# A mixture of 32 experts in another order: 64 slots from place 8 on, heavy and light groups in turn, the last scatter behind the branch

## The chip, the core and the metric

The kernel runs on one core of a Trainium2 chip, as one program in one launch. The metric is the time of one execution on the device in microseconds; the median of a few executions is quoted. Profiles show one execution, with times counted from its first instruction.

## What is computed

One layer of a decoder trunk on 256 tokens of width 1024: an attention mixer, a normalisation, then a mixture of experts and a second normalisation. All data are 32-bit floats. The change lies in the mixture:

```python
def moe_ffn(h, router_w, router_b, w_gu, b_gu, w_down, b_down):
    tok = h.reshape(Bn * S, D)                     # 256 x 1024
    logits = (tok @ router_w + router_b)           # 256 x 32
    top_v, top_i = lax.top_k(logits, TOP_K)        # 4 of 32 experts
    top_w = jax.nn.softmax(top_v, axis=-1)
    combine = jnp.sum(jax.nn.one_hot(top_i, N_EXPERTS) * top_w[..., None], axis=1)
    for e in range(N_EXPERTS):
        gu = tok @ w_gu[e] + b_gu[e]               # 1024 x 2048
        gate = jnp.minimum(gu[:, 0::2], SWIGLU_LIMIT)
        up = jnp.clip(gu[:, 1::2], -SWIGLU_LIMIT, SWIGLU_LIMIT)
        act = (up + 1.0) * (gate * jax.nn.sigmoid(SWIGLU_ALPHA * gate))
        out = out + combine[:, e:e + 1] * (act @ w_down[e] + b_down[e])   # 1024 x 1024
    return out
# x = layer_norm(DN_ALPHA * x + (1.0 + gate) * moe_ffn(...), ln2_g, ln2_b)
```

The 1024 pairs of token and expert are spread unevenly. With the reference's drawn inputs, experts 0 and 1 get 18 and 2 tokens, and the other thirty, sorted by count, get 84, 82, 70, 69, 68, 65, 55, 46, 42, 41, 38, 34, 33, 31, 31, 29, and then from 25 down to 6.

## The kernel before

**Weights.** Every expert has 12 MB of weights, which `Stream` loads as 12 units of 1 MB, each into one buffer of 128 x 2048 floats (`Stream.unit`, L121). All loads are issued on SP's queue, in the order in which the experts are computed. In the mixture the buffers are taken in turn from the list `ROUND`, which names 3 + 2 + 5 + 4 + 1 + 1 + 1 = 17 of them (`FIRST`, `ROUND`); the four of `PARTS` are those that `W.place` gives. A load waits on SP until TensorE has done with the unit that the same buffer held 17 loads earlier.

**Slots and places.** The tokens of one expert are gathered into slots, whose number is fixed when the program is built. Experts 0 and 1 are computed first, with 64 slots each (group `G0`). The others are sorted on the chip by their token counts: place 2 is the fullest. `slots_of(p)` gives a place 128, 64 or 32 slots: class `Wide` for places 2 to 8 (`WIDE = 9`), `Narrow` for 9 to 15, `Few` for 16 to 31. A `Wide` expert streams each weight column through the whole array, a `Narrow` one runs two products beside each other on half of the columns, a `Few` one four on a quarter each. If any expert has more tokens than slots, a flag is set (`order[32]`), and behind the last expert all engines enter the branch `tc.If(more[0] > 0)` (L1711), which computes the experts once more for the tokens left over. Otherwise they jump over it.

**Groups.** Two experts make a group, which gathers its tokens together (`Group.gather`, four times four products from `xr` through `sel`, while the group before it is still computed), and turns and weighs its slots (`slots`, `weights`). Within a group the second member is computed first. A *heavy* group is one `Wide` and one `Narrow` place, a *light* one two `Few` places. `sweep` walks through 24 steps for each expert; tables of steps (`first`, `side`, `turn`) hold what is done beside the weight products. The order of the groups is written out:

```python
groups = [G0]
for heavy in (0, 1, 1, 0, 1, 1, 0, 1, 1, 0, 1, 0, 0, 0, 0):
```

TensorE, SP and GpSimd issue in the order of the program text, and so do VectorE and ScalarE in the mixture.

**The end.** Each expert's result is scaled by its weights (`weigh`, to `y`) and added by a product with `selT` to the sums `acc` in PSUM (`scatter`, on step 25 counted from the expert's start). Before the last expert, `first_sum` moves the sums so far, scaled by one plus the gate, into `x1`; the last expert starts the sums afresh and is scaled by the gate in `weigh` (`late`, `first_of_all`). The gate and the two rows of the last normalisation are spread over 128 partitions by small products with a row of ones (`spread_row`, `keep_row`) into two of the buffers of `W.place`, which `W.keep` takes out of the list. Behind the branch VectorE adds `acc` to `x1` (L1734) and the last normalisation follows.

Of the kernel before, what the change touches and what calls it, by code (L numbers as in the profile page):

```python
# [17 lines left out]
D = 1024  # L18
# [9 lines left out]
WIDE = 9  # L28
# [51 lines left out]
class Stream:  # L80
# [4 lines left out]
    def __init__(self, nc, pool, ahead):  # L85
# [4 lines left out]
        self.small = None  # L90
# [7 lines left out]
    def keep(self):  # L98

        many = len(self.others)  # L100
        at = next(j for j in ((self.turn + i) % many for i in range(many)) if self.others[j] == self.place)
        self.others = self.others[:at] + self.others[at + 1:]
        self.turn = (self.turn - (at < self.turn)) % len(self.others)
        return self.place()

    def buffer(self):
        if self.others:
            get = self.others[self.turn]
            self.turn = (self.turn + 1) % len(self.others)
            return get()  # L110
        return self.raw()
# [65 lines left out]
def body(tc, A, taps=None):  # L177
# [4 lines left out]
    with ctx:  # L182
# [1007 lines left out]
        class Group:  # L1190
# [12 lines left out]
            def choose(self, engine=POOL):  # L1203
                self.X = [s15("X", (128, 2, 192)) for _ in range(4)]
                self.sel = s2("sel", (128, 2, 256))
                self.selT = [s1("selT", (128, 256)) for _ in self.members]
# [67 lines left out]
        acc = []  # L1274

        class Expert:
# [16 lines left out]
            def weigh(self, y, t, n=None):  # L1293

                z = t2k("y")
# [111 lines left out]
        def late(expert):  # L1407

            return isinstance(expert.key, tuple) or expert.key == experts[-1].key

        def first_of_all(expert):
            return expert.key in (0, experts[-1].key)
# [82 lines left out]
        def sweep(experts, total, base):  # L1495

            for t in range(total + 2):
# [6 lines left out]
                run(turn, t)  # L1504
# [123 lines left out]
        groups = [G0]  # L1628
        for heavy in (0, 1, 1, 0, 1, 1, 0, 1, 1, 0, 1, 0, 0, 0, 0):
            groups.append(Group(pq, [by[128 if heavy else 32].pop(0), by[64 if heavy else 32].pop(0)]))  # L1630
        assert not any(by.values())
        places = [(G, s) for G in groups for s in reversed(range(len(G.members)))]
# [35 lines left out]
        def keep_row(j, n):  # L1668
            b = spread_row(j, n)
            if n == 0 and j != 7:  # L1670
                spread_rows["8" if j == 8 else "67"] = W.keep()
            spread_rows[j] = spread_rows["8" if j == 8 else "67"][:, (j == 7) * D:(j == 7) * D + D]
            spread_rows["g2z"] = spread_rows["8"][:, D:D + 512]
# [155 lines left out]
```

## Time and profile before

| what | us |
|---|---|
| median of 3 runs | 1309.14 |
| fastest and slowest of them | 1307.37 and 1318.86 |
| the profiled execution | 1315.57 |
| its span, first to last instruction | 1313.8 |
| TensorE busy in the span | 1199.0 |
| mixture, first weight product to last | 287.7 to 1295.5 |

The profile's page gives the busy time of each engine, the span in 40 slices, the DMA queues, the chain of work that ended last, and the costliest groups of instructions. Beside the page, the trace was read by windows: the busy time of each engine, the granted TensorE clock (1.00 is 2.4 GHz, 0.50 is 1.2 GHz) and the DMA rate in a stretch. The stretches used here begin and end with the first weight product of a group, so their length is what TensorE took for that group.

### The profile page before, as it was taken

Reading aid. Unit: us, or ns where it says so; the run is one execution under the profiler, and the core shown is the slowest. Engines: PE = TensorE matmul, PEld = TensorE weight load, DVE = VectorE, ACT = ScalarE, POOL = GpSimd, SP = SyncE. Lnnn points to the kernel's source line nnn. Section 1 sums busy time; section 2 is a strip of 40 time slices with the busy share of each in tenths; the row PEclk is TensorE's granted clock in tenths of the full one; section 3 lists DMA queues with packets and bytes.
Section 4 is the critical chain, followed back from the end, with each engine's and each line's share of the span. In section 5 each row is a group of like instructions: output and inputs, shape, how many; then the busy total and the mean of one; then the engine's idle time right before and its main releaser. Section 6 shows DMA issues by size and latency. Waiting matters only on the chain. (4 is left out here: it accounts for less than half of the span.)

```text
span 1313.8 us, 16305 instructions
## 1 busy us (share of the span) xinstructions
PE 1199.0 (91%) x6200; PEld 628.7 (48%) x6200; DVE 405.8 (31%) x937; ACT 277.3 (21%) x546; POOL 90.7 (7%) x120
## 2 busy tenths in 40 slices
PE   6989999989999999988999988999988998787783
PEld 6878888874333444533443533453433353232220
DVE  7898778742122111211111201121211121110023
ACT  4655545331111110111111111111111111110011
POOL 0014620000000000000000000000000000000000
PEclk9999999978999999988999999999999999898887
DMA  9986766929999999799999889999889999999993
GB/s 381 347 334 248 265 222 257 365 83 418 416 420 421 421 421 411 268 374 421 420 370 385 285 340 421 421 414 369 306 319 420 420 420 395 421 420 420 422 417 152
DMA packets 69814, 474.63 MB, mean 361 GB/s; under 512 B 9645, under 2 KB 10346, under 8 KB 13920
## 3 DMA queue, kind: packets, MB, share of 16 engines
q1 hardware_dynamic: 68288, 469.28, 88.9%
q0 software_dynamic: 1296, 3.97, 0.9%
q8 instruction: 51, 0.84, 0.3%
q14 instruction: 35, 0.29, 0.1%
q10 hardware_dynamic: 144, 0.26, 0.1%
HBM read 472.41 MB, written 3.43 MB: 362 GB/s over the span
## 5 line engine op out<-in xcount | busy, mean ns | idle before, releaser
L194 PE MATMUL b<-raw,X 128*32 128x512 f32 (+2 forms) x2048 | 470.1, 608 | 14.1 <-DMA raw<-in_wexp 14.0
L194 PE MATMUL b<-raw,an 128*32 128x512 f32 (+2 forms) x1024 | 256.4, 715 | 43.7 <-DVE an L1388 25.5
L194 PEld LDWEIGHTS b<-raw,X 128*32 128x32 f32 (+2 forms) x2048 | 150.1, 135 | 265.8 <-issue 230.1
L194 PEld LDWEIGHTS b<-raw,an 128*32 128x32 f32 (+2 forms) x1024 | 80.5, 149 | 172.7 <-issue 137.1
L1228 DVE TENSOR_SCALAR X<-b,G,B 128x64 f32<-128x64 f32 (+2 forms) x64 | 26.0, 406 | 412.0 <-ACT X L1230 412.0
L194 PE MATMUL b<-hh,hi 128*128 128x256 f32 x336 | 97.5, 290 | 12.6 <-ACT hh L326 12.6
L1177 POOL TENSOR_SCALAR sel<-cst,pq 128x128 f32<-128x128 f32 x60 | 37.1, 634 | 932.5 <-PE b L1307 489.9
L194 PEld LDWEIGHTS b<-sel,xr 128*128 128x128 f32 x512 | 77.5, 201 | 47.2 <-issue 44.7
L194 PE MATMUL b<-hh,lo 128*128 128x256 f32 x336 | 94.8, 282 | 1.5 <-DVE lo L158 1.3
L194 PE MATMUL b<-hl,hi 128*128 128x256 f32 x336 | 94.7, 282 | 0.8 <-DVE hl L327 0.7
L1230 ACT ACTIVATE X<-b,B,G 128x64 f32<-128x64 f32 (+2 forms) x64 | 29.1, 454 | 278.3 <-PE b L194 278.3
L194 PE MATMUL b<-sel,xr 128*128 128x64 f32 (+2 forms) x512 | 85.6, 313 | 0.2 <-DVE sel L1177 0.2
L194 PE MATMUL b<-y,selT 64*128 64x512 f32 (+1 forms) x256 | 75.7, 611 | 4.3 <-ACT y L1301 3.4
L1287 DVE TENSOR_TENSOR gm<-b,biasT 128x256 f32<-128x256 f32 (+1 forms) x48 | 24.0, 501 | 178.8 <-PE b L1307 178.8
L158 DVE TENSOR_TENSOR lo<-raw,hi 128x1024 fp32r<-128x1024 f32 (+1 forms) x58 | 70.0, 1222 | 9.7 <-ACT hi L147 9.7
L194 PEld LDWEIGHTS b<-hh,hi 128*128 128x128 f32 x336 | 64.7, 192 | 14.6 <-ACT hh L326 12.6
L147 ACT ACTIVATE hi<-raw 128x1024 fp32r<-128x1024 f32 (+1 forms) x58 | 59.6, 1046 | 33.8 <-PE b L194 25.8
L194 PEld LDWEIGHTS b<-hh,lo 128*128 128x128 f32 x336 | 64.8, 193 | 2.5 <-DVE lo L158 1.7
L1255 DVE COPY wsl<-b 128x2 f32<-128x2 f32 x16 | 2.5, 159 | 204.9 <-PE b L194 204.9
L194 PEld LDWEIGHTS b<-hl,hi 128*128 128x128 f32 x336 | 64.5, 192 | 1.4 <-DVE hl L327 1.3
L1301 ACT ACTIVATE y<-b,wsl 128x512 f32<-128x512 f32 x38 | 26.1, 687 | 146.2 <-PE b L194 146.2
L1307 PEld LDWEIGHTS b<-cst,gu 128*128 128x128 f32 x248 | 28.6, 143 | 52.0 <-ACT gu L1484 26.8
(306 smaller groups left out, 1043.5 us busy)
## 6 DMA issues: line engine op xcount, KB each, us to landing
raw<-in_wexp SPq DMA_DIRECT2D x384, 1024.0 KB, 16.2
raw<-in_wmg SPq DMA_DIRECT2D x12, 1024.0 KB, 4.8
raw<-in_moda SPq DMA_DIRECT2D x8, 1024.0 KB, 7.2
raw<-in_modg SPq DMA_DIRECT2D x8, 1024.0 KB, 5.4
raw<-in_modf SPq DMA_DIRECT2D x8, 1024.0 KB, 5.1
raw<-in_wg SPq DMA_DIRECT2D x8, 752.0 KB, 7.7
raw<-in_cw SPq DMA_DIRECT2D x4, 1024.0 KB, 7.2
raw<-in_wbr SPq DMA_DIRECT2D x4, 1024.0 KB, 6.8
```

The costliest lines, as they stand in the source:

```text
L147: self.nc.scalar.activation(part[1][:, :m], src, AF.Copy)
L158: self.nc.vector.tensor_sub(part[2][:, :m], src, hi[:, :m].bitcast(F32))
L194: PE.matmul(out, x, w, start=start, stop=stop, skip_group_check=True, **kw)
L1177: engine.tensor_scalar(out, iota, src[:, i, p:p + 1], None, op0=OP.is_equal)
L1228: V.tensor_scalar(x, v, G2[:, k], B2[:, k], op0=OP.mult, op1=OP.add)
L1230: ACT.activation(x, v, AF.Identity, bias=B2[:, k], scale=G2[:, k])
L1255: at(side, t + 2, lambda: V.tensor_copy(self.wsl[:, 0:n], b[:, 0:n]))
L1287: V.tensor_tensor(v, z, bias[:, :, None].to_broadcast(shape), OP.add)
L1301: at(side, t, lambda: ACT.activation(z, y, AF.Copy, scale=w))
L1307: PE.transpose(z[:, j * 128:(j + 1) * 128], gu[:, j * 128:(j + 1) * 128], C("ident"))
```

## The change

`WIDE` becomes 8: place 8 gets 64 slots in place of 128. There are now six heavy groups and a group of two `Narrow` places, which stands behind `G0`. Then a heavy and a light group alternate six times, and the last two light groups follow. The last expert's `scatter` is left out of the sweep and issued behind the branch; its operands lie in tiles of their own (`selTl`, and part of a kept buffer for `z`). `first_sum` comes one expert earlier, so that the last two experts are the late ones, and the small products for the rows move with it. `W.keep` now asks for two buffers at step `end - 92`, and `buffer` gives them when the turn comes to one of `W.place`, where before `keep` took the next one out of turn, at steps `end - 30` and `end - 24`.

```diff
-WIDE = 9
+WIDE = 8
...
-    def keep(self):
-        many = len(self.others)
-        at = next(j for j in ((self.turn + i) % many for i in range(many)) if self.others[j] == self.place)
-        self.others = self.others[:at] + self.others[at + 1:]
-        self.turn = (self.turn - (at < self.turn)) % len(self.others)
-        return self.place()
+    def keep(self, n):
+        self.want, self.kept = n, []
...
     def buffer(self):
         if self.others:
             get = self.others[self.turn]
+            while self.want and get == self.place:
+                self.want -= 1
+                self.kept.append(get())
+                self.others = self.others[:self.turn] + self.others[self.turn + 1:]
+                self.turn %= len(self.others)
+                get = self.others[self.turn]
...
-                z = t2k("y")
+                z = W.kept[1][:, D + 512:] if self.key == experts[-1].key else t2k("y")
...
-            return isinstance(expert.key, tuple) or expert.key == experts[-1].key
+            return isinstance(expert.key, tuple) or expert.key in (experts[-2].key, experts[-1].key)
...
-            return expert.key in (0, experts[-1].key)
+            return expert.key in (0, experts[-2].key)
...
-        groups = [G0]
-        for heavy in (0, 1, 1, 0, 1, 1, 0, 1, 1, 0, 1, 0, 0, 0, 0):
-            groups.append(Group(pq, [by[128 if heavy else 32].pop(0), by[64 if heavy else 32].pop(0)]))
+        groups = [G0, Group(pq, [by[64].pop(0), by[64].pop(0)])]
+        while by[32]:
+            if by[128]:
+                groups.append(Group(pq, [by[128].pop(0), by[64].pop(0)]))
+            groups.append(Group(pq, [by[32].pop(0), by[32].pop(0)]))
...
-        at(first, end - 36, load_rows)
+        at(first, end - 60, load_rows)
+        at(first, end - 92, lambda: W.keep(2))
...
-                plan_rows((end - 30 + 2 * n) if j == 8 else (end - 26 + 4 * n + 2 * m), keep_row, j, n)
+                plan_rows((end - 54 + 2 * n) if j == 8 else (end - 36 + 4 * n + 2 * m), keep_row, j, n)
             for i in range(2):
-                at(side, end - 16 + 2 * i + 4 * n, lambda i=i, n=n: first_sum(i, n))
+                at(side, end - 40 + 2 * i + 4 * n, lambda i=i, n=n: first_sum(i, n))
...
-        sweep(experts, end, W.at[0, 0])
+        sweep(experts, end, W.at[0, 0], end + 1)
+        last_scatter = turn.pop(end + 1)
...
+        for f in last_scatter:
+            f()
```

What TensorE issues shows it at three places. In the rows, `raw,X` are the products with the first weight matrix, `raw,an` those with the second, and 128, 64 or 32 ahead of `x512` is the number of slots; `sel,xr` is a gather, `cst,sel` and `pqw,sel` turn and weigh the slots, `cst,gu` turns an expert's middle result, `y,selT` is a scatter, `rows,cst` spreads a row.

TensorE of before, from the last scatter of `G0` on, where the first light group begins:

```order
L194 MATMUL b<-y,selT 128x512 x4
L194 MATMUL b<-raw,X 32x512 x8
L1239 MATMUL b<-cst,sel 128x128 x4
L194 MATMUL b<-raw,X 32x512 x8
L194 MATMUL b<-pqw,sel 128x1 x4
L194 MATMUL b<-raw,X 32x512 x16
L194 MATMUL b<-rows,cst 128x512
L1307 MATMUL b<-cst,gu 128x128 x4
```

TensorE of the change at the same place, where the group of two `Narrow` places begins:

```order
L196 MATMUL b<-raw,X 64x512 x4
L196 MATMUL b<-y,selT 128x512 x4
L196 MATMUL b<-raw,X 64x512 x8
L1242 MATMUL b<-cst,sel 128x128 x4
L196 MATMUL b<-raw,X 64x512 x4
L196 MATMUL b<-pqw,sel 128x1 x4
L196 MATMUL b<-raw,X 64x512 x4
L1311 MATMUL b<-cst,gu 128x128 x4
L196 MATMUL b<-raw,X 64x512 x12
L196 MATMUL b<-rows,cst 128x512
```

The products with 32 slots at this place have become products with 64, and the row products stand among them as before.

TensorE of before, at the end of the first `Wide` expert: its scatter, and the next heavy group begins with its `Narrow` member.

```order
L194 MATMUL b<-raw,an 128x512 x6
L194 MATMUL b<-sel,xr 128x192 x4
L194 MATMUL b<-raw,an 128x512 x8
L194 MATMUL b<-y,selT 128x512 x2
L194 MATMUL b<-raw,X 64x512 x4
L194 MATMUL b<-y,selT 128x512 x2
L194 MATMUL b<-raw,X 64x512 x8
L1239 MATMUL b<-cst,sel 128x128 x4
```

TensorE of the change, at the end of its first `Wide` expert:

```order
L196 MATMUL b<-raw,an 128x512 x6
L196 MATMUL b<-sel,xr 128x64 x4
L196 MATMUL b<-raw,an 128x512 x8
L196 MATMUL b<-y,selT 128x512 x4
L196 MATMUL b<-raw,X 32x512 x8
L1242 MATMUL b<-cst,sel 128x128 x4
L196 MATMUL b<-raw,X 32x512 x8
L196 MATMUL b<-pqw,sel 128x1 x4
```

A light group now follows where a second heavy one did, and the gather ahead of it is 64 columns wide in place of 192.

TensorE of before, from the end of the sweep into the branch:

```order
L194 MATMUL b<-raw,X 32x512 x24
L1307 MATMUL b<-cst,gu 128x128 x4
L194 MATMUL b<-raw,an 32x512 x16
L194 MATMUL b<-y,selT 128x512 x4
L1711 COMPARE_AND_BRANCH
```

TensorE of the change, the same end:

```order
L196 MATMUL b<-raw,X 32x512 x32
L1311 MATMUL b<-cst,gu 128x128 x4
L196 MATMUL b<-raw,an 32x512 x16
L1720 COMPARE_AND_BRANCH
```

and behind the branch:

```order
L1720 UNCONDITIONAL_BRANCH x2
L196 MATMUL b<-raw,selTl 128x512 x4
L1837 UNCONDITIONAL_BRANCH
```

The four products of the last scatter have moved from ahead of the branch to behind it. VectorE's row for the last `y` still stands ahead of the branch.

## Rows read from the trace of the kernel before

**Rows 1.** The page's 40 slices of 32.8 us: what DMA moved.

```profile
GB/s 381 347 334 248 265 222 257 365 83 418 416 420 421 421 421 411 268 374 421 420 370 385 285 340 421 421 414 369 306 319 420 420 420 395 421 420 420 422 417 152
```

**Rows 2.** Windows by groups: length, busy times; last three: clock, DMA share, GB/s.

```profile
287.70:359.20 71.50, 70.08 (x339) 30.09 (x338) 15.41 (x54) 9.33 (x20) 5.00 (x8) 0.93 0.97 397
359.20:403.80 44.60, 39.87 (x262) 15.16 (x260) 11.33 (x25) 5.41 (x11) 0.00 (x0) 0.92 1.01 420
403.80:430.90 27.10, 26.40 (x129) 9.19 (x125) 4.75 (x13) 3.37 (x7) 2.44 (x4) 1.00 1.01 421
403.80:562.30 158.50, 157.10 (x564) 70.29 (x560) 26.93 (x58) 21.14 (x39) 7.54 (x12) 1.00 0.95 385
562.30:607.20 44.90, 38.25 (x255) 15.10 (x254) 6.46 (x17) 5.42 (x11) 0.00 (x0) 0.85 0.96 395
607.20:765.70 158.50, 157.11 (x566) 70.28 (x562) 26.94 (x58) 21.14 (x39) 7.55 (x12) 1.00 0.93 366
765.70:808.40 42.70, 36.06 (x253) 15.00 (x252) 6.45 (x17) 5.42 (x11) 0.00 (x0) 0.92 0.96 392
808.40:967.00 158.60, 157.20 (x568) 70.34 (x568) 26.94 (x58) 21.14 (x39) 7.55 (x12) 1.00 0.94 371
967.00:1009.70 42.70, 36.06 (x255) 15.08 (x254) 6.45 (x17) 5.42 (x11) 0.00 (x0) 0.92 0.96 395
1009.70:1088.90 79.20, 78.50 (x288) 34.75 (x284) 13.27 (x29) 10.70 (x20) 4.78 (x8) 1.00 1.01 420
1088.90:1133.50 44.60, 37.11 (x261) 14.15 (x260) 5.93 (x17) 5.68 (x12) 2.33 (x4) 0.89 0.97 401
1133.50:1177.20 43.70, 36.34 (x265) 13.65 (x263) 5.93 (x17) 5.67 (x12) 2.33 (x4) 0.92 1.01 421
```

**Rows 3.** TensorE's waits in 403.8 to 1100, all of them.

```profile
PE b L194 <- DVE an L1388: 12.4, 10, 2.5
PE b L194 <- issue: 7.6, 3, 2.5
PE b L1307 <- ACT gu L1484: 5.6, 7, 0.8
```

**Rows 4.** SP's longest wait in 403.8 to 1100: us, times, longest.

```profile
SPq L121 <- PE b L194: 382.1, 155, 6.0
```

**Rows 5.** TensorE's longest wait in 1133.5 to 1296.

```profile
PE b L194 <- DMA raw<-in_wexp: 14.0, 12, 2.1
```

**Rows 6.** Timeline of TensorE in the first light group and the heavy group behind it.

```profile
368.08 1.12 PE L194 MATMUL b<-rows,cst 9*128 9x512 f32 x2
369.13 0.66 PE L1307 MATMUL b<-cst,gu 128*128 128x128 f32 x4
...
386.58 1.57 PE L194 MATMUL b<-sel,xr 128*128 128x192 f32 x8
388.08 1.92 PE L194 MATMUL b<-raw,X 128*32 128x512 f32 x16
...
411.17 0.66 PE L1239 MATMUL b<-cst,sel 128*128 128x128 f32 x4
411.76 1.94 PE L194 MATMUL b<-raw,X 128*64 128x512 f32 x8
413.62 1.05 PE L194 MATMUL b<-pqw,sel 128*128 128x1 f32 x8
414.61 1.94 PE L194 MATMUL b<-raw,X 128*64 128x512 f32 x8
```

**Rows 7.** Timeline of the end: start, us, engine, line.

```profile
1295.62 0.75 DVE L1299 SCALAR_TENSOR_TENSOR y<-b,wsl,raw 128x512 f32<-128x512 f32 x1 [6.84 <-PE b L194]
...
1296.42 1.99 PE L194 MATMUL b<-y,selT 64*128 64x512 f32 x8 [0.90 <-DVE y L1299]
...
1301.32 0.69 DVE L1734 SCALAR_TENSOR_TENSOR raw<-b,x 128x512 f32<-128x512 f32 x1 [4.95 <-issue]
```

**Rows 8.** Line 1711, the branch: ns, first and last start.

```profile
L1711 PEldq COMPARE_BRANCH  x1: 3751/3751/3751, 1296.4 to 1296.4; - x1
L1711 PEldq EVENT_SEMAPHORE  x1: 51/51/51, 1300.3 to 1300.3; - x1
```

**Rows 9.** The chain that ended last, in order of time: start, us, what.

```profile
1299.07 2.06 issue
```

More of the change, by code (lines that the diff above doesn't have):

```diff
@@ L88, in __init__ @@
         self.others, self.turn = [], 0
-        self.small = None
+        self.small, self.want, self.kept = None, 0, []
     def half(self, kind):
@@ L1205, in choose @@
                 self.sel = s2("sel", (128, 2, 256))
-                self.selT = [s1("selT", (128, 256)) for _ in self.members]
+                self.selT = [q.tile([128, 256], F32, name="selTl") if self.members[s][0] == last_place[0] and not self.past
+                             and s == 0 else s1("selT", (128, 256)) for s in range(len(self.members))]
                 self.wsl = q.tile([128, 2], F32, tag="wsl", name="wsl", bufs=2)
@@ L1272, in plan @@
                 at(turn, t + 31, lambda: self.weights(t + 31))
-        acc = []
+        acc, last_place = [], [None]
         class Expert:
@@ L1493, in body, with sweep @@
         KIND = {128: Wide, 64: Narrow, 32: Few}
-        def sweep(experts, total, base):
+        def sweep(experts, total, base, leave=None):
             for t in range(total + 2):
@@ L1503, in sweep @@
                     experts[t // 24].step(t % 24)
-                run(turn, t)
+                if t != leave:
+                    run(turn, t)
         G0 = Group(pp, [(1, 64), (0, 64)])
@@ L1626, in body @@
         by = {n: [(p, n) for p in range(FIXED, NE) if slots_of(p) == n] for n in KIND}
-        groups = [G0]
-        for heavy in (0, 1, 1, 0, 1, 1, 0, 1, 1, 0, 1, 0, 0, 0, 0):
-            groups.append(Group(pq, [by[128 if heavy else 32].pop(0), by[64 if heavy else 32].pop(0)]))
+        groups = [G0, Group(pq, [by[64].pop(0), by[64].pop(0)])]
[3 more added lines that the diff above has]
+            groups.append(Group(pq, [by[32].pop(0), by[32].pop(0)]))
         assert not any(by.values())
+        last_place[0] = groups[-1].members[0][0]
         places = [(G, s) for G in groups for s in reversed(range(len(G.members)))]
@@ L1669, in keep_row @@
             b = spread_row(j, n)
[L1670 to L1673, printed above, removed]
+            spread_rows[j] = W.kept[j == 8][:, (j == 7) * D:(j == 7) * D + D]
+            spread_rows["g2z"] = W.kept[1][:, D:D + 512]
             def out():
@@ L1712, in body @@
             rest = [([(p, 128)], 64 + n * 128) for p in range(FIXED) for n in range(2)]
-            rest += [([(p, 128)], 128) for p in range(FIXED, WIDE)]
-            for a, b, n in ((WIDE, NARROW, 64), (NARROW, NE, 32)):
+            rest += [([(p, 128)], 128) for p in range(FIXED, WIDE)] + [([(WIDE, 128)], 64)]
+            for a, b, n in ((WIDE + 1, NARROW, 64), (NARROW, NE, 32)):
                 rest += [([(q, n) for q in range(p, min(p + 2, b))], n) for p in range(a, b, 2)]
```

## Prediction

> **What bounds the kernel now.** I read the slices first. From slice 10 on, DMA moves 416 to 422 GB/s, its full rate here, except in dips to 268, 285, 306 and 319 [rows 1]. So the mixture is limited by DMA in most slices, and something holds DMA up in the others. Next I read windows cut at the groups [rows 2]. In the row of `G0`, 71.5 us long, `G0` is computed; 359.2 to 403.8 is the first light group with the row products in it; the rows of 158.5, 158.5 and 158.6 us are two heavy groups each; the 79.2 us from 1009.7 is the seventh heavy group alone; the rows of 44.9, 42.7 and 42.7 us are the light groups that stand between heavy ones. Heavy groups are dense: TensorE is busy all but 0.7 us in each `Narrow` member, the clock is 1.00, and a group costs the same 79.2 us in each of them. The rest of the mixture, from 1088.9 on, is four light groups.
>
> The two resources have these prices. A unit is 1024 KB, and at 421 GB/s that takes 2.49 us; an expert of 12 units takes 29.9 us, a group 59.8 us. TensorE needs 79.2 us for a heavy group, 19.4 more than its data, and 43.4 us (the mean of 44.9, 42.7 and 42.7) for a light one, 16.4 less. A run of heavy groups makes DMA fill all 17 buffers and then wait for TensorE: the pairs of heavy groups show 385, 366 and 371 GB/s [rows 2], and SP's longest wait there is for TensorE, 382.1 us [rows 4]. TensorE itself waits for no load at all from 403.8 to 1100; its few waits are for the middle results [rows 3]. From 1133.5 on it is the other way round: DMA runs at 421 GB/s, and TensorE's longest wait is for loads [rows 5]. So up to the last heavy group TensorE sets the pace, and behind it DMA does.
>
> What DMA loses follows from the rates: length times (421 - rate) / 421 over the windows gives 4.1 in `G0`, 13.6, 20.7 and 18.8 in the three pairs of heavy groups, 2.8, 2.9 and 2.6 in the light groups between them, 0.2 in the seventh heavy group, 2.1 behind it and 0.1 in the first light group: 67.9 us, of which 63.8 behind `G0` [rows 2]. That is the most which any order of groups can win.
>
> **The order of the groups.** The point from which DMA alone decides is the end of the last heavy group. I work out when TensorE gets there. Before: `G0`, one light group with the rows (44.6), seven heavy, three light (130.3 together), which ends at 1088.9. After: `G0`, the two `Narrow` places, six heavy, five light.
>
> The pair of `Narrow` places has no row of its own. One `Narrow` member takes 27.1 us [rows 2]; in it stand the turning of slots, 0.59, and their weights, 0.99 (start to next start) [rows 6], and one scatter. The first of the two also gets the four row products, 1.05 each [rows 6]: 27.1 + 4.2 = 31.3. The second has no slots to turn or weigh, and the gather of the heavy group behind it, four pieces of 1.50 [rows 6]: 27.1 - 1.6 + 6.0 = 31.5. Together 62.8 us. The least is 54.2, two members as they stand with all else hidden; the most I put at 67, by four more waits of the middle results like those of [rows 3], about 1 us each. I take the sum of the pieces, since a heavy group leaves only 0.7 us idle to hide them in.
>
> So the last heavy group ends at 1088.9 - 44.6 + 62.8 - 79.2 + 2 x 43.4 = 1114.7, which is 25.8 us later than before. But then only three light groups are left, not four: 24 units fewer, 24 x 2.49 = 59.8 us, since DMA sets the pace there. The rest of the span, 1313.8 - 1088.9 = 224.9, becomes 165.1. **Sum: +25.8 - 59.8 = -34.0 us.**
>
> This needs all 17 buffers full at the end of the last heavy group, as they are at 1088.9. A heavy and a light group together take TensorE 122.6 us and DMA 119.6, so in each of the six turns DMA is held up for about 3 us. The trace has such a turn: the seventh heavy group comes behind a light one, and it and the light group after it lose 0.2 + 2.1 us [rows 2]. The first heavy group will hold DMA up longer: by the rates of [rows 2], DMA brings 27.1 units in `G0` and would bring 25.2 in the 62.8 us of the `Narrow` pair, 52.3 for the 48 used, against 45.0 before. It thus starts the heavy group 7.3 units further ahead. Two heavy groups in a row took it from the old start to the full ring, 2 x 7.8 units less the 13.6 us (5.5 units) held up, that is 10.1; now one takes it from 7.3 to 15.1, so it is held up 5.0 units, 12.5 us. With five turns of 3 us and the 4.1 of `G0`, DMA loses about 32 us in place of 67.9: 36 saved, which agrees with the 34 from TensorE's side.
>
> **The end.** The last scatter now stands behind the branch. Before, the last `y` is ready at 1296.37, the scatter runs from 1296.42 for 1.99 us, and VectorE adds at 1301.32 [rows 7]. The scatter had long ended. What ends last is 2.06 us from 1299.07 in which VectorE waits for nothing that the profile shows, behind its own jump [rows 9]; this jump, and the `y` ahead of it, stay where they were. TensorE's branch took 3.75 us from 1296.4, and it was past it at 1300.3 [rows 8]. Moved ahead of the scatter, it can start beside the last weight products, and the scatter would follow at about 1298 to 1299 and end by 1301. I cost this edit at nothing: VectorE's own jump hides it. The Trainium skill speaks against such an edit: its page "Runtime: NRT & Kernel Launch", section "Instruction fetch mechanics", says that a jump to code outside the small window already fetched stalls the engine until that code has come. The pauses behind the branch on VectorE and TensorE agree with that; by the page the scatter too could meet such a second pause. If TensorE meets one like VectorE's 2.06, the scatter ends near 1303 and the end comes up to 2.1 us later; if VectorE had after all waited for TensorE to be past the branch, about 1 us is won. So -1 to +2.1.
>
> **The kept buffers.** The ring loses two of its 17 buffers at about unit 342 of 384, not at 372. It costs nothing where TensorE is the faster one, which it is from the last heavy group on: that group ends with unit 312 used and unit 329 the last that the full ring lets in; while the 13 units to 342 come, in 32 us, TensorE uses 18 (24 in 43.4 us), so 12 buffers hold data and 15 suffice. If the ring were still full then, two units would come late, 5 us. `first_sum`, the row products and their copies move into light groups that wait for DMA; they cost nothing there (the first light group took them for 44.6 us, as long as others without). The two late experts' `y` moves from ScalarE to VectorE, 0.75 us [rows 7], on an idle engine.
>
> **Time.** In its own execution: 1315.57 - 34.0 = 1281.6. That execution lay 6.4 us above the median, and 1.8 us lie outside its span; I carry the difference over: 1309.1 - 34.0 = **1275**. Bounds: the `Narrow` pair -8.6 to +4.2; the five light groups, against 217.0 in the sum, 213.5 at 42.7 each or 224.5 at 44.9, -3.5 to +7.5; the end -1 to +2.1; the ring 0 to +5. All at their ends: 1262 to 1294.
>
> **Rivals.**
> 1. *DMA never waits again.* If a heavy and a light group together took 119.6 us or less, the whole 63.8 would be won: 1245. It needs light groups of 40.4 us; 42.7 is the least seen [rows 2]. Against it also the clock, already 1.00 in heavy groups. 4 in 100.
> 2. *Half of the gain.* The light groups, now each between two heavy ones, cost 46 rather than 43.4 (2.6 x 5 = 13) by more waits like those in [rows 3]: -21, 1288. The dearest seen is 44.9. 10 in 100.
> 3. *The clock falls, and it is slower.* Light groups have the lower granted clock, 0.85 to 0.92 against 1.00 [rows 2], and there are more of them among the heavy ones. If all five ran at 0.50, their 36.06 us of busy time at 0.92 would become 66 and each would take 30 more: +150, to about 1425. It decides at 34.0 / 5 = 6.8 us per light group, that is 50.2. The Trainium skill has this rule ("TensorE: Matmul & The Clock Gate", section "HAM oscillation — how this bites in real kernels"): where the work between two waits for data is short, the engine falls back to the half clock again and again. The rows show only a little of it in light groups where no load is waited for. 2 in 100.
> 4. *The smaller number of slots doesn't hold.* If place 8 had over 64 tokens, the branch would be entered, with 34 more passes of 12 units: 408 x 2.49 = 1016, to about 2290. With the drawn inputs it has 55. 1 in 100.
> 5. *Only the end of the ring counts*: the kept buffers and the end at their dear ends, the `Narrow` pair above 67 by waits that no row shows: within 13 of before. 3 in 100.
>
> The forecast has the remaining 80 in 100, and the range with rival 2's time inside it is 1262 to 1292. A measurement of this kernel tells 1% from no change, 13 us, since its runs spread by 11. Faster by more than that: the forecast and rivals 1 and 2, 0.94. Slower: rivals 3 and 4, 0.03.
>
> **What would show it.** The window of the `Narrow` pair is 60 to 66 us long; the heavy groups stay at 79.2 and the light ones between them at 42.7 to 44.9; a heavy and a light group together show DMA near 411 GB/s (119.6 / 122.6 of 421), the first heavy group 350 to 360; the last heavy group ends near 1115; behind it DMA runs at 420 to the end, and VectorE's first add stands some 4 to 6 us behind the last `y`. The prediction is wrong if TensorE waits for loads between heavy groups, if light groups take over 46, or if VectorE's add waits for the scatter.

## The result and the profile after

The change is faster: 1263.36 us (median of 4 runs, 1262.39 to 1272.21) against 1311.86 for the kernel before in the same runs (1307.37 to 1318.86). The ratio is 0.964, with an interval of 0.958 to 0.971, so 3.6% are won. The forecast was 1275, with a range of 1262 to 1292: the time lies in the range, 1.4 us above its low end. The profiled execution took 1263.40 us and its span is 1261.6, 52.2 less than before; between the medians it is 48.5, between the fastest runs 45.0. Three of the four runs lie within 1.0 us of the fastest and the fourth is 9.8 us above it, so a difference of a few us is read from profiles here, not from medians.

The page's slices of the kernel after, 31.5 us each, show what DMA moved.

```profile
GB/s 379 345 323 288 265 220 291 279 159 351 414 418 419 421 420 343 421 420 421 395 421 421 420 413 419 423 420 395 421 420 413 389 420 421 378 423 420 418 421 182
```

In the mixture before there were three stretches of dips, down to 268, 285 and 306, two to four slices each, under the three pairs of heavy groups [rows 1]. Now, behind the start of `G0` and up to the last slice, 343 and 378 are the lowest, each by itself.

Windows of the kernel after, cut at the groups as in [rows 2], with the same columns (length, busy times; last three: clock, DMA share, GB/s). In their order: `G0`, the `Narrow` pair, the first heavy group, the light group behind it, the second heavy, a light one, three later light ones, the sixth and last heavy, the light group behind it, and the last two light groups together.

```profile
285.60:349.50 63.90, 63.27 (x331) 27.44 (x332) 15.47 (x54) 8.87 (x19) 2.66 (x4) 1.00 0.96 393
349.50:410.80 61.30, 61.30 (x280) 23.25 (x278) 16.11 (x37) 8.13 (x16) 2.44 (x4) 1.00 1.01 420
410.80:490.00 79.20, 78.50 (x290) 34.70 (x287) 13.27 (x29) 10.70 (x20) 4.78 (x8) 1.00 0.99 403
490.00:532.60 42.60, 36.02 (x255) 14.49 (x254) 6.46 (x17) 5.42 (x11) 0.00 (x0) 0.92 0.96 395
532.60:611.80 79.20, 78.50 (x288) 34.73 (x284) 13.23 (x29) 10.70 (x20) 4.79 (x8) 1.00 1.01 420
611.80:652.90 41.10, 34.52 (x255) 13.97 (x254) 6.46 (x17) 5.41 (x11) 0.00 (x0) 0.96 0.97 400
732.10:774.80 42.70, 36.11 (x253) 14.78 (x252) 6.45 (x17) 5.41 (x11) 0.00 (x0) 0.92 1.01 414
854.10:897.70 43.60, 37.02 (x255) 14.97 (x254) 6.46 (x17) 5.41 (x11) 0.00 (x0) 0.88 0.97 403
976.90:1020.60 43.70, 37.12 (x255) 15.05 (x254) 6.45 (x17) 5.41 (x11) 0.00 (x0) 0.88 0.96 398
1020.60:1099.80 79.20, 78.50 (x288) 34.71 (x284) 13.28 (x29) 10.70 (x20) 4.77 (x8) 1.00 1.01 418
1099.80:1143.40 43.60, 36.21 (x261) 13.61 (x260) 5.93 (x17) 5.67 (x12) 2.33 (x4) 0.92 0.96 396
1143.40:1242.80 99.40, 77.40 (x474) 24.43 (x476) 16.53 (x39) 12.75 (x27) 0.00 (x0) 0.93 1.00 413
```

A heavy group costs 79.2 us as before. What changed is what DMA does meanwhile: the three pairs of heavy groups lost it 13.6, 20.7 and 18.8 us [rows 2], the single ones lose 3.4 at most in this profile. By the prediction's reckoning, length times (421 - rate) / 421, all windows from 285.6 to 1143.4 together lose 21.5 us, where those of before lost 67.9.

TensorE's waits between 410.8 and 1099.8, all of them, and SP's longest (us in total, times, longest):

```profile
PE b L196 <- DVE an L1392: 16.7, 11, 2.5
PE b L196 <- issue: 12.7, 5, 2.5
PE b L1311 <- ACT gu L1488: 7.7, 10, 0.8
```

```profile
SPq L123 <- PE b L196: 298.1, 131, 5.8
```

They answer to [rows 3] and [rows 4]. TensorE still waits for no load there. It waits for its own middle results, and for 12.7 us the profile names no cause ("issue"); both come more often than before, since five light groups stand there where three did. SP's wait for TensorE fell from 382.1 to 298.1.

The timeline of the end (start, us, engine, line), and two rows of the branch, line 1720 here (ns, first and last start): TensorE's jump, and the first thing that VectorE records on that line behind its own jump.

```profile
1245.77 0.75 DVE L1303 SCALAR_TENSOR_TENSOR raw<-b,wsl,raw 128x512 f32<-128x512 f32 x1 [5.06 <-PE b L196]
1247.17 1.99 PE L196 MATMUL b<-raw,selTl 64*128 64x512 f32 x8 [1.48 <-PEq L1720]
1249.16 0.69 DVE L1746 SCALAR_TENSOR_TENSOR raw<-b,x 128x512 f32<-128x512 f32 x1 [2.64 <-PE b L196]
```

```profile
L1720 PEldq COMPARE_BRANCH  x1: 3622/3622/3622, 1243.4 to 1243.4; - x1
L1720 DVEq EVENT_SEMAPHORE  x1: 21/21/21, 1248.7 to 1248.7; - x1
```

From the start of the last `y` to VectorE's first add it was 5.70 us before [rows 7] and is 3.39 now. TensorE passes its branch while the last weight products run, and the add now starts as soon as the scatter ends, 0.5 us after VectorE is past its own jump.

### The profile page after: what moved, and what is told of

Its sections match the earlier page's. It is cut to its first block, busy times and chain, and to the rows that moved or that the text cites. A ratio compares the mean times of both kernels' runs of the same rounds, so it can differ in the third digit from the quotient of the medians.

```text
span 1261.6 us, 16290 instructions
## 1 busy us (share of the span) xinstructions
PE 1156.2 (92%) x6192; PEld 608.0 (48%) x6192; DVE 404.2 (32%) x938; ACT 273.5 (22%) x542; POOL 89.8 (7%) x120
## 5 line engine op out<-in xcount | busy, mean ns | idle before, releaser
L196 PE MATMUL b<-raw,X 128*32 128x512 f32 (+2 forms) x2048 | 449.0, 600 | 10.0 <-DMA raw<-in_wexp 9.9
L196 PE MATMUL b<-raw,an 128*32 128x512 f32 (+2 forms) x1024 | 241.9, 687 | 43.1 <-DVE an L1392 23.7
L196 PEld LDWEIGHTS b<-raw,X 128*32 128x32 f32 (+2 forms) x2048 | 141.8, 133 | 249.9 <-issue 218.7
L196 PEld LDWEIGHTS b<-raw,an 128*32 128x32 f32 (+2 forms) x1024 | 75.2, 144 | 166.8 <-issue 131.9
L196 PE MATMUL b<-hh,hi 128*128 128x256 f32 x336 | 97.3, 290 | 12.7 <-ACT hh L328 12.7
L196 PEld LDWEIGHTS b<-sel,xr 128*128 128x128 f32 x512 | 74.5, 197 | 48.4 <-issue 45.9
L196 PE MATMUL b<-sel,xr 128*128 128x64 f32 (+2 forms) x512 | 82.8, 306 | 0.2 <-DVE sel L1179 0.2
L196 PE MATMUL b<-y,selT 64*128 64x512 f32 (+1 forms) x248 | 71.3, 611 | 2.5 <-ACT y L1305 1.6
L196 PEld LDWEIGHTS b<-hh,hi 128*128 128x128 f32 x336 | 64.2, 191 | 14.4 <-ACT hh L328 12.7
```

Of the source, the lines that this page charges most:

```text
L196: PE.matmul(out, x, w, start=start, stop=stop, skip_group_check=True, **kw)
```

## The experiments

Theory A, the prediction's: the order of the groups decides. TensorE sets the pace up to the last heavy group, DMA behind it, and two heavy groups in a row are what makes DMA stop. Theory B, the rival: the smaller slots decide, since 64 instead of 128 at place 8 take work from TensorE, and the order only distributes it. Smaller questions were the end, the kept buffers and the depth of the ring. Each comparison has the kernel before measured on the same chip in the same rounds: 1312.73 us for the kernels with the order alone, the slots alone, two heavy groups in a row and the scatter ahead, 1311.55 for the other four. The change itself has its one set of runs, beside 1311.86; differences from it are taken between sets in which the kernel before differs by up to 1.2 us.

**The order alone**, in the kernel before (`WIDE` stays 9; first a heavy, then a light group, seven times):

```diff
-        for heavy in (0, 1, 1, 0, 1, 1, 0, 1, 1, 0, 1, 0, 0, 0, 0):
-            groups.append(Group(pq, [by[128 if heavy else 32].pop(0), by[64 if heavy else 32].pop(0)]))
+        while by[32]:
+            if by[128]:
+                groups.append(Group(pq, [by[128].pop(0), by[64].pop(0)]))
+            groups.append(Group(pq, [by[32].pop(0), by[32].pop(0)]))
```

> The kernel before with the order of groups alone changed: G0, then a heavy and a light group in turn seven times, then the last light group (place 8 keeps 128 slots; end and kept buffers as before). Theory A (the order decides, since DMA is held up only while heavy groups follow each other): the last heavy group ends at 287.7 + 71.5 + 7 x 79.2 + 4.2 (row products) + 6 x 42.7 = 1174, and two light groups are left, 224.9 - 119.6 = 105.3: span near 1279, 34 us under before, nearly all of the change's gain. Theory B (the gain is the TensorE work saved at place 8): only the rest is won here, 48 - 25 = 23 us or less. Theory C (the order is worth nothing): 0.

Measured: 1273.2 us (1271.38 to 1274.34), ratio 0.970 (0.967 to 0.973), 39.5 less than before. Its windows of the first heavy group and of all that follows the last one, to the end of the span:

```profile
358.30:441.30 83.00, 83.00 (x298) 35.73 (x298) 18.34 (x37) 10.71 (x20) 4.79 (x8) 1.00 0.93 369
1166.50:1271.00 104.50, 75.35 (x501) 25.62 (x500) 25.32 (x59) 18.07 (x35) 0.00 (x0) 0.86 0.82 335
```

The heavy group behind `G0` holds DMA up (369 GB/s); it also has the row products, hence 83.0. The last heavy group ends 77.6 us later than before, at 1166.5 against 1088.9, yet the whole is shorter, since two light groups are left behind it instead of four. The reordering alone brings four fifths of what the change does. TensorE's waits behind the last heavy group, all of them:

```profile
PE b L194 <- DVE an L1388: 5.0, 2, 2.5
PE b L194 <- issue: 4.0, 2, 2.5
PE b L1307 <- ACT gu L1484: 3.1, 4, 0.8
PE b L194 <- DVE y L1299: 0.9, 1, 0.9
PE b L194 <- ACT y L1301: 0.8, 1, 0.8
```

None is for a load, so here TensorE sets the pace to the end, and DMA is through before it (335 GB/s). The 9.8 us that the change has on this kernel are then to be sought in TensorE's work at place 8, in the end, and in what differs between executions; no run separates them.

**The slots alone**, in the order of before, with the seventh heavy group replaced by the `Narrow` pair:

```diff
-WIDE = 9
+WIDE = 8
...
-        for heavy in (0, 1, 1, 0, 1, 1, 0, 1, 1, 0, 1, 0, 0, 0, 0):
-            groups.append(Group(pq, [by[128 if heavy else 32].pop(0), by[64 if heavy else 32].pop(0)]))
+        for a, b in ((32, 32), (128, 64), (128, 64), (32, 32), (128, 64), (128, 64), (32, 32), (128, 64), (128, 64),
+                     (32, 32), (64, 64), (32, 32), (32, 32), (32, 32), (32, 32)):
+            groups.append(Group(pq, [by[a].pop(0), by[b].pop(0)]))
...
```

> The kernel before with 64 slots at place 8 alone; the seventh heavy group becomes a pair of Narrow places at the same seat, the order is otherwise kept. Theory A: from 967 on DMA runs without a pause, as it nearly did before, so only the 2.3 us that it lost around the seventh heavy group are won: 0 to 3 us faster. Theory B: 22 to 25 us faster, the TensorE work saved (a Wide member takes 52.2, a Narrow one 27.1).

Measured: 1311.2 us (10 runs, 1306.53 to 1318.77), ratio 0.999 (0.996 to 1.001). The pair's window:

```profile
1015.10:1073.70 58.60, 57.11 (x284) 21.63 (x282) 10.52 (x29) 8.39 (x17) 4.77 (x8) 1.00 1.01 420
```

TensorE is done with the pair in 58.6 us, 20.6 sooner than with the heavy group, and nothing of it reaches the end: behind the last heavy pair DMA runs at its rate (420) and has as many units left as before. Theory B falls for this order.

**Two heavy groups in a row again**, in the change (`G0`, the `Narrow` pair, then two heavy and two light in turn):

```diff
         while by[32]:
-            if by[128]:
-                groups.append(Group(pq, [by[128].pop(0), by[64].pop(0)]))
-            groups.append(Group(pq, [by[32].pop(0), by[32].pop(0)]))
+            for _ in range(2):
+                if by[128]:
+                    groups.append(Group(pq, [by[128].pop(0), by[64].pop(0)]))
+            for _ in range(2):
+                groups.append(Group(pq, [by[32].pop(0), by[32].pop(0)]))
```

> The change with the same groups in another order: behind the Narrow pair two heavy and two light groups in turn three times, then two light ones. Theory A: TensorE reaches the end of the last heavy group one light group (42.7) earlier than in the change, but four light groups are left, 59.8 more: 17 us slower than the change, span near 1279, and the second heavy group of each pair shows DMA near 310 to 330 GB/s. Theory B (only the amount of TensorE work counts): the same as the change.

Measured: 1296.55 us (1286.9 to 1298.77), ratio 0.986 (0.981 to 0.992); 33 of the change's 48 are gone, nearly twice what was expected. The second heavy group of each pair:

```profile
495.50:574.80 79.30, 78.60 (x285) 34.77 (x286) 13.13 (x29) 10.01 (x19) 5.10 (x8) 1.00 0.86 326
743.80:823.10 79.30, 78.60 (x283) 34.76 (x283) 13.13 (x29) 10.02 (x19) 5.10 (x8) 1.00 0.96 389
990.50:1069.70 79.20, 78.50 (x281) 34.70 (x280) 13.13 (x29) 10.01 (x19) 5.10 (x8) 1.00 0.98 398
```

The mechanism is the expected one: DMA is held up in each second heavy group, the windows up to the first light group behind the last heavy one lose it 49 us instead of the change's 21.5, and the last heavy group ends at 1069.7 with four light groups left, 223.7 us to the end of the span. Its size per pair was wrong: only the first pair, which starts with the lead from `G0` and the `Narrow` pair, shows the 310 to 330 GB/s that were expected for all. The expectation also had the end of the last heavy group about 13 us earlier: the mixture started 2.3 us later in this execution than in the change's, `G0` took 3.3 more and the two pairs of light groups about 7 more.

**A light group ahead of each heavy one**, in the change (`G0`, the `Narrow` pair, six times light and heavy, two light):

```diff
         while by[32]:
+            groups.append(Group(pq, [by[32].pop(0), by[32].pop(0)]))
             if by[128]:
                 groups.append(Group(pq, [by[128].pop(0), by[64].pop(0)]))
-            groups.append(Group(pq, [by[32].pop(0), by[32].pop(0)]))
```

> The change with the alternation begun by a light group: G0, the Narrow pair, then light and heavy in turn six times, then two light ones. Theory A: the first heavy group no longer starts with the ring far ahead, so DMA isn't held up for the 17 us that it lost there; TensorE reaches the end of the last heavy group 42.7 later than in the change, but two light groups are left, 59.8 fewer: 17 us faster than the change, near 1246, with TensorE and DMA ending nearly together. If the light groups at the end are what gives the gain (they were made last on purpose): 10 us or more slower than the change.

Measured: 1255.29 us (6 runs, 1249.47 to 1258.72), ratio 0.956 (0.953 to 0.959): 8 less than the change, and all six runs lie below the change's fastest. Its windows of the first heavy group and the light one behind it, of the last heavy group, and of the last two light groups:

```profile
464.10:543.40 79.30, 78.60 (x292) 34.80 (x289) 13.29 (x29) 10.70 (x20) 4.78 (x8) 1.00 1.01 420
543.40:586.00 42.60, 36.01 (x253) 14.49 (x252) 6.46 (x17) 5.42 (x11) 0.00 (x0) 0.92 1.01 420
1070.90:1150.10 79.20, 78.50 (x288) 34.71 (x284) 13.28 (x29) 10.70 (x20) 4.78 (x8) 1.00 0.98 408
1150.10:1194.70 44.60, 38.23 (x265) 14.21 (x264) 6.65 (x19) 7.85 (x16) 0.00 (x0) 0.92 0.95 386
1194.70:1240.80 46.10, 38.74 (x230) 10.68 (x228) 9.88 (x21) 6.33 (x12) 0.00 (x0) 0.85 0.92 381
```

The `Narrow` pair and `G0` let DMA run ahead, so a heavy group straight behind them finds the ring nearly full; a light group in between uses that lead up first, and DMA keeps 420 through the first heavy and light group. I had expected 9 us more. The last heavy group ends at 1150.1 instead of 1142.5: the mixture starts 4.8 us later in this execution than in the change's, `G0` takes 6.5 more and the `Narrow` pair 1.0, and the six light groups are 5 us shorter than the sum had them. With only two light groups left DMA no longer decides the end: TensorE waits for a load once, for 1.7 us, behind 1150.

**The same order with 128 slots at place 8** (the kernel just shown, `WIDE = 9`, no `Narrow` pair):

```diff
-WIDE = 8
+WIDE = 9
...
-        groups = [G0, Group(pq, [by[64].pop(0), by[64].pop(0)])]
+        groups = [G0]
...
```

> The order of the run with the light group first, but 128 slots at place 8 and no Narrow pair: G0, then light and heavy in turn seven times, then one light group. In the old order the 64 slots were worth 1.5 us. Theory A: once the order leaves DMA unheld, TensorE is what is left, so now they count: the last heavy group ends near 287.7 + 71.5 + 4.2 + 7 x 79.2 + 7 x 42.7 = 1217, the last light group and the end add 42.7 + 18.3: near 1278, 30 us slower than the run with 64 slots. If slots are worth nothing in any order: the same as that run.

Measured: 1280.09 us (1275.82 to 1286.56), ratio 0.978 (0.974 to 0.982), 24.8 more than with 64 slots. The seventh heavy group, and what follows it:

```profile
1136.30:1218.00 81.70, 81.00 (x292) 35.17 (x288) 14.67 (x31) 12.98 (x24) 2.45 (x4) 1.00 0.94 380
1218.00:1274.00 56.00, 36.29 (x237) 10.95 (x236) 18.81 (x41) 9.31 (x18) 0.00 (x0) 0.85 0.48 196
```

Here DMA is through early (196 GB/s in the last 56 us) and TensorE has the last heavy group still ahead of it at 1136.3: TensorE's work decides, and the slots count in full. So B is not wrong in itself. The slots are worth 1.5 us in the old order and 24.8 in this one; what they are worth is set by who is late at the end. The same holds for the order: with 128 slots at place 8, light groups first took 1280.09 us where heavy groups first, with the old end, took 1273.2 (the order alone, above). A light group ahead of each heavy one wins nothing there, where TensorE is late anyway.

**A ring of 13 buffers instead of 17**, in the change (one of the `W.raw` buffers in place of five):

```diff
-        ROUND = FIRST + of(1, lambda: s8((128, 2048), "raw"))
+        ROUND = (of(3, lambda: p8("raw", (128, 2048))) + of(2, lambda: s8((128, 2048), "raw"))
+                 + of(1, W.raw) + of(PARTS, W.place)
+                 + of(1, lambda: p8("raw", (128, 2048))) + of(2, lambda: s8((128, 2048), "raw")))
```

> The change with 13 buffers in the ring of the mixture in place of 17 (four of the five general buffers left out of it). Theory A: with heavy and light in turn the ring swings by some 9 units, so 13 still keep TensorE fed; only the lead at the end of the last heavy group is 4 units shorter, 4 x 2.49 = 10 us slower than the change. If the depth of the ring sets what is lost in each turn: 6 x 10 = 60 us slower.

Measured: 1273.85 us (1271.84 to 1282.17), ratio 0.973 (0.970 to 0.977), 10.5 more than the change. Its first heavy group, and all behind the last one to the end of the span:

```profile
414.10:493.30 79.20, 78.50 (x290) 34.70 (x290) 13.28 (x29) 10.69 (x20) 4.78 (x8) 1.00 0.89 353
1097.90:1271.20 173.30, 126.53 (x761) 41.10 (x760) 32.04 (x77) 22.83 (x46) 2.33 (x4) 0.87 0.90 372
```

The last heavy group ends as early as in the change, 1097.9 against 1099.8, and the rest takes 173.3 instead of 161.8. Four units fewer can lie ready at that point, which leaves 4 x 2.49 = 10.0 us more of loading for the end. Nothing like 60 us is lost, so 13 buffers do for the turns themselves. That is the prediction's condition ("this needs all 17 buffers full") seen from its other side.

**The kept buffers out of turn at once**, in the change: out of turn, as the kernel before took them, but both at step `end - 56`, without waiting for the turn to come to them:

```diff
     def keep(self, n):
-        self.want, self.kept = n, []
+        for _ in range(n):
+            many = len(self.others)
+            at = next(j for j in ((self.turn + i) % many for i in range(many)) if self.others[j] == self.place)
+            self.others = self.others[:at] + self.others[at + 1:]
+            self.turn = (self.turn - (at < self.turn)) % len(self.others)
+            self.kept.append(self.place())
...
-        at(first, end - 92, lambda: W.keep(2))
+        at(first, end - 56, lambda: W.keep(2))
```

> The change with the two kept buffers taken out of turn and at once, as before, at step end - 56. Predicted cost of that part was nothing: the same as the change within 3 us, all theories alike; a difference over 5 us would show that the kept buffers matter. It also shows G0 once more: 34.5 us for its first member and 32.7 for its second if the half clock stands in the first one alone.

Measured: 1263.02, 1263.71, 1274.25 and 1274.42 us, ratio 0.969 (0.965 to 0.973). The change's own runs lie as far apart (1262.39 and 1272.21), so the median says nothing about 3 us. The profiled spans are 1261.3 and, for the change, 1261.6. `G0`, the first heavy group, the light group behind it, and all behind the last heavy group:

```profile
287.50:354.70 67.20, 66.57 (x331) 29.28 (x332) 15.53 (x54) 8.86 (x19) 2.67 (x4) 0.95 0.97 395
416.00:495.20 79.20, 78.50 (x290) 34.70 (x287) 13.28 (x29) 10.70 (x20) 4.78 (x8) 1.00 0.96 386
495.20:536.20 41.00, 34.41 (x253) 13.94 (x252) 6.46 (x17) 5.41 (x11) 0.00 (x0) 0.96 0.95 394
1099.80:1261.30 161.50, 121.73 (x761) 41.52 (x760) 32.05 (x77) 22.83 (x46) 2.33 (x4) 0.86 0.90 373
```

Behind the last heavy group, where the buffers are taken, it is 161.5 us and 161.8 in the change: no difference seen. `G0` is 67.2 us, 34.5 in its first member and 32.7 in its second, as expected for a stretch of the half clock in the first one alone; the change's profile had 31.2 and 32.7.

**The last scatter ahead of the branch**, in the change:

```diff
-        sweep(experts, end, W.at[0, 0], end + 1)
-        last_scatter = turn.pop(end + 1)
+        sweep(experts, end, W.at[0, 0])
+        last_scatter = []
```

> The change with the last scatter again ahead of the branch, nothing else. In the trace of the change the first add of the end stands 2.6 us behind the last y, before it was 4.95. If the move of the scatter won that: 2.3 us slower than the change, with VectorE's pause of 2 us behind its jump or a wait for TensorE's branch back in the trace. If the pause of before hung on where the code lies: no difference, 2.6 us again.

Measured: 1264.93 us (1264.63 to 1277.83), ratio 0.967 (0.961 to 0.973), with 1265.02 in the profiled execution against the change's 1263.40. Its timeline of the end, and the two rows of the branch:

```profile
1245.94 0.75 DVE L1303 SCALAR_TENSOR_TENSOR raw<-b,wsl,raw 128x512 f32<-128x512 f32 x1 [6.57 <-PE b L196]
1246.75 1.99 PE L196 MATMUL b<-raw,selTl 64*128 64x512 f32 x8 [0.86 <-DVE raw L1303]
...
1250.77 0.69 DVE L1746 SCALAR_TENSOR_TENSOR raw<-b,x 128x512 f32<-128x512 f32 x1 [4.08 <-PEq L1720]
```

```profile
L1720 PEldq COMPARE_BRANCH  x1: 3858/3858/3858, 1246.8 to 1246.8; - x1
L1720 DVEq EVENT_SEMAPHORE  x1: 21/21/21, 1248.8 to 1248.8; - x1
```

The scatter runs earlier, and the add later: TensorE gets to its branch only when the scatter is issued, at 1246.8, is past it 3.9 us later, and the profile names that branch as what VectorE's add waited for; VectorE itself was past its own jump at 1248.8. From the last `y` to the add it is 4.83 us, 1.44 more than in the change.

**Both kernels once more**, one execution each beside one of the kernel before (1309.69), to see what of a profile belongs to the kernel and what to the execution.

> The kernel before, looked at once more, as a control: the executions of one kernel spread by 10 to 12 us, and the profiled one of before lay high (1315.6, mean granted clock 0.951). If that spread is the clock: the heavy groups are 79.2 again, and the time differs from 1315.6 only in G0, in light groups and at the end, lower with a higher mean clock. If it is DMA: the rate behind the last heavy group differs from 420 GB/s.

> The change, looked at once more, as a control: its profiled execution had no half clock in the first member of G0 (31.2 us; 34.5 in most other runs). If that is chance: 34.5 or 31.2 here, the sum of the Narrow pair and the heavy groups as before, and the first add 3.4 us behind the start of the last y again.

Measured: 1320.89 us for the kernel before, 1272.21 for the change. `G0` and the first light group of the kernel before:

```profile
289.60:362.70 73.10, 71.69 (x341) 30.58 (x340) 15.30 (x54) 9.34 (x20) 5.01 (x8) 0.91 0.97 396
362.70:411.90 49.20, 44.48 (x264) 16.40 (x262) 11.41 (x25) 5.42 (x11) 0.00 (x0) 0.83 1.01 420
```

The heavy groups are 79.2 or 79.3 us again. The mixture starts 1.9 us later than in the first profile, `G0` takes 1.6 more and the light group with the rows 4.6, of which the next light group takes 2.5 back. So the difference does lie in `G0` and light groups, but it isn't told by the mean clock, which is 0.952 here and was 0.951 in the shorter execution.

Of the change, `G0`, the first heavy group, and all behind the last heavy one:

```profile
283.10:353.60 70.50, 69.88 (x333) 29.97 (x334) 15.60 (x54) 8.87 (x19) 2.67 (x4) 0.90 0.97 396
414.80:494.00 79.20, 78.51 (x286) 34.70 (x282) 13.28 (x29) 10.71 (x20) 4.79 (x8) 1.00 0.93 369
1108.50:1270.50 162.00, 118.55 (x761) 39.05 (x760) 32.01 (x77) 22.84 (x46) 2.34 (x4) 0.91 0.89 367
```

`G0` at a clock of 0.90 takes 6.6 us more than at 1.00. With it the first heavy group holds DMA up for longer (369 GB/s, 9.8 us by the same reckoning, instead of 3.4), and it makes up 6.6 of the 11.2 us by which TensorE is later to the end of the last heavy group (825.4 us after the mixture's start against 814.2); the light groups have the rest, 43.6 or 43.7 each instead of 42.7 on average. The first member of `G0` takes 34.5 us here, the second 36.0; the `Narrow` pair takes 61.2, and VectorE's first add stands 3.53 us behind the start of the last `y`.

## Why the prediction came out as it did

**What bounds the kernel** was read rightly. The order alone brings 39.5 us, the slots alone 1.5, where the interval (0.996 to 1.001) allows for nothing at all, two heavy groups in a row take 33 back, and a ring of 13 costs the 10 us that four missing units cost. Nothing of this fits an account by TensorE's work alone.

**The order of the groups** had the right mechanism, and its sum was 18.2 us short of the profiled spans' difference. The last heavy group was to end at 1114.7 and ended at 1099.8, 14.9 sooner:

| step up to there | costed | profiled | difference |
|---|---|---|---|
| start of the mixture | 287.7 | 285.6 | -2.1 |
| `G0` | 71.5 | 63.9 | -7.6 |
| `Narrow` pair | 62.8 | 61.3 | -1.5 |
| six heavy groups | 475.6 | 475.3 | -0.3 |
| five light groups | 217.0 | 213.7 | -3.3 |

(0.1 is rounding.) The heavy groups and the pair came out as costed. What was costed too dear are `G0` and the light groups, the stretches in which the granted clock falls below 1.00. Their cost was taken from the one profile there was, and it differs from execution to execution. Three more profiles show it, of kernels that do the same as the change up to the last heavy group:

| profile | `G0` | five light groups | mixture's start to the end of the last heavy group |
|---|---|---|---|
| forecast | 71.5 | 217.0 | 827.0 |
| the change | 63.9 | 213.7 | 814.2 |
| buffers out of turn at once | 67.2 | 208.3 | 812.3 |
| scatter ahead of the branch | 67.2 | 208.4 | 812.1 |
| the change again | 70.5 | 218.3 | 825.4 |

One of the four came out as forecast, to 1.6 us, and three 13 to 15 us sooner. The light groups were given a lower bound of 213.5, and two profiles lie 5 below it, with groups of 41.0 us at a clock of 0.96, where the one profile had shown 42.7 at least; `G0` and the start of the mixture were given no bound. That the measured time still lies in the range, near its low end, is in part luck. In three profiles of kernels that keep the old order `G0` took 71.5, 73.1 and 73.1 us; whether the change has a share in its shorter `G0` isn't shown. On the side of the kernel before stands the first light group, costed at 44.6 from the one profile: it took 49.2 in the second, so removing it was worth up to 4.6 more. Behind the last heavy group 165.1 was forecast; the two profiles have 161.8 and 162.0, some 3 less, of which 2.2 to 2.3 is the end. DMA moved 396 GB/s in the first light group there and 413 in the last two, not 420 throughout.

The first heavy group was to show 350 to 360 GB/s. It showed 403, 386, 387 and 369 where `G0` took 63.9, 67.2, 67.2 and 70.5 us. By the prediction's reckoning that is 3.4, 6.6, 6.4 and 9.8 us of DMA held up: the longer `G0`, the further DMA is ahead, about one us for each. So the step from `G0`'s lead to a ring that overflows was right in kind. Carried on to a `G0` of 71.5 us, the row gives 10.8 (an estimate) where 12.5 was costed; the rest of the miss is `G0`'s own.

**The end** is the step that failed: "I cost this edit at nothing: VectorE's own jump hides it", with -1 as the best end. It won 2.3 us, and two things had to come together for it. One is VectorE's pause of 2.06 us [rows 9]. In the kernel before, VectorE was past its jump here:

```profile
L1711 DVEq EVENT_SEMAPHORE  x1: 21/21/21, 1298.8 to 1298.8; - x1
```

The first add came 2.5 us later, and so it did in the three other profiles with the old end. In seven profiles with the scatter behind the branch it comes 0.5 us later. With the scatter ahead in the changed code it comes at 1250.77, sooner than 2.5 us behind VectorE's 1248.8, so the pause is gone there too; why it went isn't shown. Its going brings the end from 5.70 to 4.83 us, 0.87 less, and no further, since then the add waits for TensorE to be past its branch, as the profile names it. The other thing is the move of the scatter. It lets TensorE reach its branch about 3 us earlier and brings the end from 4.83 to 3.39, 1.44 less. Had the pause stayed, the move would have won little: 1248.7 + 2.5 = 1251.2 is 5.4 us behind the last `y`, against 5.70 (an estimate). So the price of nothing was near enough for a VectorE that pauses as before. The prediction took it to do so because its jump, and the `y` ahead of it, stay where they were, and that didn't hold. An add that waits for the scatter, which the prediction named as a sign against itself, did come in the change, but costs hardly anything: in three of the other profiles the add waits for VectorE's own jump instead, and stands 3.39 to 3.50 us behind the last `y`. The Trainium skill ("Runtime: NRT & Kernel Launch", "Instruction fetch mechanics") agrees in part: TensorE stands 3.62 us in its branch here and 3.86 with the scatter ahead. The second pause that by that page the scatter might have met isn't in the trace: the scatter starts at 1247.17, directly behind the branch.

**The kept buffers** show no cost: whether they are taken in turn or at once makes no difference, and behind the last heavy group the change took no longer than forecast. What the ring loses by having two buffers fewer was not run by itself.

**The rivals.** DMA that never waits (rival 1) didn't come: it needed light groups of 40.4 us, and the shortest between heavy groups took 41.0. The order with light groups first came nearer to it, at 1255.29 against 1245. Dearer light groups (rival 2) didn't come: 41.1 to 43.7 against the 46 that it needed. The falling clock (rival 3) neither: the five light groups have 0.88 to 0.96, and none came near 50.2 us. The Trainium skill's rule behind it ("TensorE: Matmul & The Clock Gate", "HAM oscillation — how this bites in real kernels") shows here only in part: the clock does fall within light groups, whose waits for middle results last up to 2.5 us, but for little of each.

## What to carry to other kernels

Where one stream of loads feeds work that is in turn shorter and longer than its data take, read off for each kind of work how much it is over or under the load time, and order it so that a ring of buffers is neither full nor empty. Where the work ahead has already filled the ring and the loads are late at the end, start with a short one. Whether less work on the engine is worth anything depends on who is late at the end: the same smaller tile brought 1.5 us in one order and 24.8 in another, so order first, then cut work, and then try the order again. The order that came out of this, light groups ahead of heavy ones, beats both the change and the kernel before at 1255.3 us with the smaller tile, and is no gain without it. A forecast to 1% needs more than one profile of every stretch whose length differs between executions.

## What the runs showed of the hardware

Executions of one program differ by more than some of the steps that are compared here, and the stretches below full clock are where. In the profiles `G0` took 63.9 us at a granted clock of 1.00, 67.2 at 0.95, 70.5 at 0.90, 71.5 at 0.93 and 73.1 at 0.91; the first light group of the kernel before took 44.6 at 0.92 and 49.2 at 0.83. A heavy group had 1.00 and 79.2 to 80.0 us everywhere, but for the two places where it also holds row products (83.0 and 81.7). The mean clock of a whole execution tells its time only roughly: the change's runs are 1262.39 to 1263.40 us at 0.966 or 0.967 and 1272.21 at 0.959, but the kernel before took 1315.57 at 0.951 and 1320.89 at 0.952. What decides whether an execution gets a stretch of the lower clock in `G0` stays open.

The jump over a branch of this size held TensorE for 3.30 to 3.86 us in the twelve profiles: 3.62 and 3.30 in two executions of the change, 3.75 [rows 8] and 3.49 in two of the kernel before. With the scatter ahead of the branch in the changed code VectorE, which needs TensorE's products, started only when TensorE was past the branch, at 1250.77, although the products themselves had ended 2 us before (1246.75 + 1.99 = 1248.74).
